# A two-layer mLSTM and latent-attention trunk: gate columns beside v, the rotary key's two parts in one weight tile, the mLSTM chunk's fp32 products by fours

## The chip, the cores and the metric

The kernel runs on one core of one Trainium2 chip. The metric is the device time of one execution in microseconds (us). Times of several executions are given as their median with the lowest and the highest.

## The reference, cut to what matters

The input is one sequence of S = 1024 tokens with D = 1024 features, all in fp32. Layer A is an mLSTM mixer (8 heads, query and key width 64, value width 128, chunks of 128 tokens) with a squared-ReLU MLP behind it. From its output comes a shared key and value: a latent of 256 features and a rotary key of 64. Layer B is latent attention over that, and an MLP again. Norms and a modulation by a conditioning vector stand around every part. The change touches two places of it, the mLSTM mixer:

```python
def mlstm_mixer(h, w_in, gate_b, head_g, w_out):
    proj = h @ w_in    # q 512, k 512, v 1024, i gate 8, f gate 8, o gate 1024 columns
    q, k, v, ig, fg, og = jnp.split(proj, splits, axis=-1)
    i_pre, f_pre = (ig + gate_b[0]), (fg + gate_b[1])
    hh = mlstm_chunkwise(q, k, v, i_pre, f_pre)
    ...
def step(carry, xs):         # one chunk of 128 tokens, per head
    ...
    s = jnp.einsum('bhtd,bhsd->bhts', qb, kb) * w_intra
    num = (w_inter[..., None] * jnp.einsum('bhtd,bhde->bhte', qb, C)   # from the state
           + jnp.einsum('bhts,bhse->bhte', s, vb))                     # within the chunk
    den = w_inter * jnp.einsum('bhtd,bhd->bht', qb, n) + jnp.sum(s, axis=-1)
    h = num / jnp.maximum(jnp.abs(den), jnp.exp(-m_t))[..., None]
```

and the rotary key of the shared latent:

```python
    kv = modulate(rmsnorm(x, g_in), shift, scale) @ w_a
    c_kv, k_rope = jnp.split(kv, [B_KV_LORA], axis=-1)    # 256 and 64 columns
    k_rope = apply_rope(k_rope, cos, sin)                 # x1 cos - x2 sin, x2 cos + x1 sin
```

## The kernel before

**Tiles and precision.** The tokens are worked in two halves of 512 (`hfs[0]`, `hfs[1]`), features on the partitions for the most part. Large products are made exact to about fp32 by splitting each operand into a rounded part `hi` and a rest `lo` and adding three products, lo by hi, hi by lo and hi by hi (`mm3`, L233 to L236). Weights are loaded by `wload`: SyncE's queue fetches 512 KB into one of four `raw` buffers (L214), ScalarE (ACT) rounds them into `wh` (L192), and VectorE (DVE) forms the rest `wl` (L193); eight `ws` buffers hold the two.

**Memory.** PSUM is shared by three pools: `ps` and `pc` with two banks each, and `pm` with two pairs of banks. In SBUF the temporaries are `tmc` (six of 512 columns), `tmp` (three) and `tma` (one), and the larger tiles `k4` (24) and `hd` (8).

**Order.** A scheduler places the instructions on in-order engine queues from the order in which they are traced. That order is woven by hand from generators: `weave` and `weave_n` run so many steps of one beside each step of another, `with_bg` runs steps of a background beside a stage, and `in_turn` alternates two streams. The background (`bgs`) computes the modulation vectors: `ada_chunk` loads 512 KB at a time into `raw` (L356) and multiplies and adds on DVE into the one `tma` tile (L361, L363). `prompt` and `tc.high_priority` move an operation ahead in the schedule, and `tc.issue_after` holds one back.

**The mLSTM's first half** (L1730 to L1742). `qk_pairs` (L572) makes q and k in four blocks of 256 features, the last of them at its end (L600 to L610), from eight weight blocks. `gates_in` (L612) then loads the 16 gate columns, spreads hi and lo over one weight tile of 128 columns (rows 0, 32 for hi and 64, 96 for lo of the result) and makes 16 products of 512 columns (L628, L629) into a `ps` bank. `gates0` (L681) adds hi and lo rows on DVE and runs a chain of some 30 short operations of DVE and ACT on eight rows: log-sigmoid, cumulative sums, running maximum, weights. `v_in` (L643) makes v with tokens on the partitions: four blocks of 256 columns, for each the two weight loads and four token tiles of 24 products of 256 columns. Beside it runs `intra0` (L743), which makes each head pair's decay weights (L754 and L757 on PE, L761 on ACT), the 64-row products of key and query (L769), their product with the weights (L774) and the scaling of q (L777 on PE, L778 on DVE).

**The chunks.** `chunks0` (L796) takes four chunks for each half. Two heads are the two row groups of 64 of one product. For each of two `pm` pairs (q), and each of its two head pairs (i), it traces two products with the state `Cst` (64 rows of contraction each, L813), then two products within the chunk (128 rows, L818), and so on alternately. The first chunk of all has no state. Behind these come the transposes of the keys (L826), the norm on ACT and DVE (L837 to L850, which frees the `pm` pair), the state's update (L861, 64 columns of output side by side) and the transposes of the result (L876). In the first half they alternate with the output gate's projection `og0` and steps of `norm0`, the second half's first norm; in the second half with `wout` of the first. `rms_x1` (L516) sums squares for that norm on ACT; the squares themselves are thrown away, into a `pc` bank.

**The second half of the mLSTM** (L1745 to L1752) runs `gates_in` with no background, then q and k in eight blocks of 128 (`qk_in`) and v, with `intra0` woven in at 0.8 steps of it to each step, and the background at 1.7.

**The rotary key.** `latent_weights` (L1133) folds gains into the latent's weights in advance, in the background, splits them, and stores hi and lo in DRAM (`lw[b, i]`); block 2 is the rotary key's 64 columns, twice side by side. `latent` (L1162) loads the blocks (`load`), makes each by `proj` (24 products of 512 columns), multiplies with the tokens' norm (`scaled`, L1212) and adds a bias (`based`, L1216). `rope` (L1113) splits block 2, multiplies by the cosines, turns the halves by two products with a permutation (L1123, L1124), multiplies by the sines and adds. The same `rope` serves the queries.

Of the kernel before, what the change touches and what calls it, by code (L numbers as in the profile page):

```python
# [9 lines left out]
F32 = mybir.dt.float32  # L10
F32R = mybir.dt.float32r
# [6 lines left out]
P = 128  # L18
# [64 lines left out]
def kernel(  # L83
# [66 lines left out]
    def pc():  # L150
        return pp.tile([P, 512], F32, tag="pc", bufs=2, name=f"pc_{next(uid)}")
# [420 lines left out]
    def qk_pairs(hf, w0, ahead):  # L572


        h = hf.h
        hf.q = [k4v(), k4v()]
        hf.k = [k4v(), k4v()]
        m0, m1 = pm(), pm()
        acc = [(m0[:, 0], m0[:, 1]), (m1[:, 0], m1[:, 1]), (ps(), ps())]

        def half(b, kh, w):
            for r in range(2):
                for k in range(4):
# [16 lines left out]
        acc.append((ps(), ps()))  # L600
        w = [w_qk(3, 0), w_qk(3, 1)]
        for r in range(2):
            for kk in range(KD):
                wk, k = w[kk // 4], kk % 4
                mm3(
                    acc[3][r], wk[0][:, k, ts(r, P)], wk[1][:, k, ts(r, P)], h.hi[kk], h.lo[kk],
                    kk == 0, kk == KD - 1,
                )
            qk_evac(hf, 6 + r, acc[3][r])
            yield  # L610

    def gates_in(hf):  # L612
        h = hf.h
        wg = raw(F32R).rearrange("p (a b) -> p a b", b=P)
        nc.gpsimd.memset(wg.bitcast(F32), 0.0)
        rg = tmp()
        rgv = rg[:, :128].rearrange("p (k n) -> p k n", n=16)
        nc.sync.dma_start(rgv, wcols(w_in, 2048, 16))
        for g in range(2):
            s = ts(g, 8)  # L620
            nc.scalar.copy(wg[:, :, 32 * g : 32 * g + 8], rgv[:, :, s])
            nc.vector.tensor_sub(
                wg[:, :, 64 + 32 * g : 72 + 32 * g], rgv[:, :, s],
                wg[:, :, 32 * g : 32 * g + 8].bitcast(F32),
            )
        gp = ps()
        for k in range(KD):
            nc.tensor.matmul(gp, wg[:, k], h.lo[k], start=k == 0, stop=False)  # L628
            nc.tensor.matmul(gp, wg[:, k], h.hi[k], start=False, stop=k == KD - 1)  # L629
        hf.gp = gp  # L630
        yield from gates0(hf)
        yield
# [9 lines left out]

    def v_in(hf):  # L643
        h = hf.h
        hf.v = []
        for t in range(4):
            v = k4().rearrange("p (h e) -> p h e", e=VE)
            nc.gpsimd.memset(v[:, :, 128:VE], 1.0)
            hf.v.append(v)
# [31 lines left out]
    def gates0(hf):  # L681
# [1 line left out]
        gp, half = hf.gp, hf.i  # L683
        r8 = lambda: tmc()[0:8]
        t1, t2, t3 = r8(), r8(), r8()
        nc.vector.tensor_copy(t1, gp[64:72])
# [109 lines left out]
    def chunks0(hf):  # L796
# [4 lines left out]
        for j in range(4):  # L801
            g = hf.i * 4 + j
            cs = ts(j, P)
            v = hf.v[j]
            nvs = []
            for q in range(2):
                num = pm()
                nv = num[:, :, 0 : 2 * VE].rearrange("p b (i e) -> p b i e", e=VE)
                for i in range(2):
                    p_ = 2 * q + i  # L810

                    for r in range(2 if g > 0 else 0):
                        nc.tensor.matmul(  # L813
                            nv[:, r, i], hf.q[p_ // 2][ts(r, 64), p_ % 2, cs],
                            Cst[ts(r, 64), p_], start=True, stop=False,
                        )
                    for r in range(2):
                        nc.tensor.matmul(  # L818
                            nv[:, r, i], hf.PT[p_][:, r, cs], v[:, 2 * p_ + r],
                            start=g == 0, stop=True,  # L820
                        )
                nvs.append(nv)
            if g < 7:
                pt = pc()
                for p_ in range(4):
# [280 lines left out]

    perm = selW[:, 0]

    def rope_perm():
        for q in range(4):  # L1110
            nc.vector.tensor_copy(perm[:, ts(q, 32)], ident[:, ts(q ^ 1, 32)])

    def rope(pt, hf, b=None):  # L1113

        hi, lo, t1 = tmc(F32R), tmc(F32R), tmc()
        split_mod(hi, lo, pt, b)
        if b is None:
            nc.vector.tensor_mul(t1, pt, hf.cs[:, 0])
        else:
            nc.vector.scalar_tensor_tensor(t1, pt, b, hf.cs[:, 0], ALU.add, ALU.mult)  # L1120
        yield
        p2 = pc()
        nc.tensor.matmul(p2, perm, lo, start=True, stop=False)  # L1123
        nc.tensor.matmul(p2, perm, hi, start=False, stop=True)  # L1124
        t2 = tmc()
        nc.vector.tensor_mul(t2, p2, hf.cs[:, 1])
        nc.vector.tensor_add(t1, t1, t2)
        return t1

# [3 lines left out]
    def latent_weights():  # L1133
# [4 lines left out]
        for b, vs in enumerate(views):  # L1138
# [19 lines left out]
            nc.vector.reduce_sum(lbias[:, b : b + 1], pt[:, :P], axis=AX.X)  # L1158

    kkd = scratch([2, P, H], "kkd")  # L1160

    def latent(hf, behind):  # L1162
# [5 lines left out]
        def load(b):  # L1168
            with tc.high_priority(PRIO):
                w = []  # L1170
                for i in range(2):
                    t = raw(F32R)
# [11 lines left out]
        def proj(b):  # L1184
            if b < 4:
                load(b + 2)
            w, pt = ready.pop(0), pc() if b == 2 else ps()
            for k in range(KD):
                mm3(pt, w[0][:, k], w[1][:, k], h.hi[k], h.lo[k], k == 0, k == KD - 1)
            return pt  # L1190

        lb = lambda b: lbias[:, b : b + 1]
# [777 lines left out]
```

## Time and profile before

| | |
|---|---|
| timed runs | 2396.66 us, median of 3 (2395.84 to 2397.26) |
| profiled execution | 2392.8 us |
| its span | 2391.0 us |
| mean granted clock of TensorE | 0.999 |
| instructions in the span | 30521 |
| HBM traffic | 313.24 MB read, 59.24 MB written |
| DMA | mean 157 GB/s |

The profile shows one execution. PE stands for TensorE's matmuls, PEld for its weight loads, DVE for VectorE, ACT for ScalarE, POOL for GpSimd, SP for SyncE and SPq for its queue of DMA issues. A row of a timeline reads: start, duration, engine, line of the kernel, operation, output and inputs by tile names, the product's rows and columns of TensorE, output or operand size, type, and how many instructions run together in that row; the brackets at its end say how long the engine had been idle and on what it waited. Records of PE overlap, since matmuls are pipelined. A granted clock of 1.00 is full speed. Busy shares are means over stages with different limits.

### The profile page before, as it was taken

The numbers are of one execution on the slowest core, as the hardware profiler recorded it, in microseconds if no ns is written. First come the engines' busy times: TensorE is split into PE (matmuls) and PEld (weight loads), VectorE is DVE, ScalarE is ACT, GpSimd is POOL, SyncE is SP. The second block draws the span as 40 slices with busy tenths as digits, with TensorE's granted clock in tenths as the row PEclk, the third lists the DMA queues.
The fourth block names the chain that finished last, engine by engine and source line by source line (L and its number), as shares of the span: only waits on it lengthen the run. The fifth ranks groups of instructions, "written<-read, shape, count | busy, mean of one in ns | idle before, by whom it ended". The sixth has DMA issues, their size and how long they took to land.

```text
span 2391.0 us, 30521 instructions
## 1 busy us (share of the span) xinstructions
PE 2365.1 (99%) x11621; PEld 1945.3 (81%) x11621; DVE 1549.9 (65%) x2431; ACT 1055.2 (44%) x1712; POOL 18.2 (1%) x91
## 2 busy tenths in 40 slices
PE   8999999999999999999999999999999999999998
PEld 5888888888888887888888878888888888888886
DVE  6667866868656677877764867766666395353345
ACT  4355334655333454444444554444444353444333
POOL 1000000000000000000000000000000000000000
PEclk9999999999999999999999999999999999999999
DMA  8442654545555745545543444774434354354431
GB/s 311 150 142 81 195 175 142 158 133 159 185 167 158 238 141 178 164 156 185 169 138 113 155 163 153 259 242 135 137 98 154 103 166 134 102 183 141 145 98 62
DMA packets 377106, 374.48 MB, mean 157 GB/s; under 512 B 24355, under 2 KB 282464, under 8 KB 376960
## 3 DMA queue, kind: packets, MB, share of 16 engines
q1 hardware_dynamic: 376672, 372.44, 49.0%
q8 instruction: 91, 1.49, 0.3%
q14 instruction: 55, 0.45, 0.1%
q0 software_dynamic: 288, 0.10, 0.0%
HBM read 313.24 MB, written 59.24 MB: 156 GB/s over the span
## 4 chain that ended last, share of the span: by engine, by line
PE 92%; DVE 3%; DMA 3%; ACT 1%; issue 1%; SPq 0%; DVEq 0%; ACTq 0%
PE ps L234 17%; PE ps L236 16%; PE ps L235 16%; PE pm L234 10%; PE pm L235 10%; PE pm L236 10%; PE pc L1448 1%; PE pc L234 1%; PE pc L235 1%; PE pc L236 1%; PE pm L1334 1%; PE pm L818 1%; DMA raw<-in_mlp_w_dram 1%; DMA raw<-in_a_w_in_dram 1%; PE pm L1328 1%
## 5 line engine op out<-in xcount | busy, mean ns | idle before, releaser
L193 DVE TENSOR_TENSOR wl<-raw,wh 128x1024 fp32r<-128x1024 f32 (+2 forms) x366 | 438.7, 1202 | 437.4 <-ACT wh L192 428.5
L192 ACT CAST wh<-raw 128x1024 fp32r<-128x1024 f32 (+2 forms) x366 | 376.3, 1032 | 708.8 <-PE ps L234 385.0
L234 PE MATMUL ps<-k,wl 128*128 128x512 f32 x1496 | 598.3, 400 | 0.9 <-DVE wl L193 0.8
L236 PE MATMUL ps<-k,wh 128*128 128x512 f32 x1496 | 588.8, 394 | 0.0
L235 PE MATMUL ps<-k,wh 128*128 128x512 f32 x1496 | 587.1, 392 | 0.0
L236 PEld LDWEIGHTS ps<-k,wh 128*128 128x128 f32 x1496 | 280.9, 188 | 66.5 <-issue 0.2
L234 PEld LDWEIGHTS ps<-k,wl 128*128 128x128 f32 x1496 | 281.0, 188 | 65.9 <-issue 2.7
L235 PEld LDWEIGHTS ps<-k,wh 128*128 128x128 f32 x1496 | 281.4, 188 | 62.2 <-issue 1.4
L201 DVE TENSOR_TENSOR k<-k,pm 128x512 f32<-128x512 f32 (+1 forms) x254 | 211.1, 859 | 107.5 <-PE pm L236 107.0
L234 PE MATMUL pm<-hd,wl 128*128 128x512 f32 x512 | 201.5, 394 | 0.4 <-ACT hd L473 0.4
L235 PE MATMUL pm<-hd,wh 128*128 128x512 f32 x512 | 199.6, 390 | 0.2 <-DVE hd L474 0.2
L236 PE MATMUL pm<-hd,wh 128*128 128x512 f32 x512 | 199.7, 390 | 0.0
L234 PE MATMUL pm<-wh,hd 128*128 128x512 f32 x488 | 193.1, 396 | 2.0 <-ACT raw L1340 1.6
L235 PE MATMUL pm<-wl,hd 128*128 128x512 f32 x488 | 191.4, 392 | 0.0
L236 PE MATMUL pm<-wh,hd 128*128 128x512 f32 x488 | 190.4, 390 | 0.0
L363 DVE SCALAR_TENSOR_TENSOR tma<-raw,cond,tma 128x512 f32<-128x512 f32 x168 | 125.6, 748 | 20.1 <-DMA raw<-in_kv_ada_w_dram 13.5
L474 DVE TENSOR_TENSOR hd<-tmp,hd 128x512 fp32r<-128x512 f32 x128 | 88.3, 690 | 57.0 <-ACT hd L473 56.7
L1340 ACT ACTIVATE raw<-pm,sm 128x128 f32<-128x128 f32 (+3 forms) x64 | 47.5, 742 | 151.3 <-DVE sm L1339 129.2
L235 PEld LDWEIGHTS pm<-hd,wh 128*128 128x128 f32 x512 | 96.2, 188 | 21.2 <-DVE hd L474 0.5
L234 PEld LDWEIGHTS pm<-hd,wl 128*128 128x128 f32 x512 | 96.1, 188 | 21.3 <-ACT hd L473 0.8
L236 PEld LDWEIGHTS pm<-hd,wh 128*128 128x128 f32 x512 | 96.1, 188 | 20.8
L960 ACT ACTIVATE tmp<-ps 128x512 f32<-128x512 f32 x128 | 75.8, 592 | 83.5 <-PE ps L236 83.4
(348 smaller groups left out, 3489.4 us busy)
## 6 DMA issues: line engine op xcount, KB each, us to landing
raw<-in_mlp_w_dram SPq DMA_DIRECT2D x256, 512.0 KB, 4.1
raw<-in_ada_w_dram SPq DMA_DIRECT2D x80, 512.0 KB, 4.4
raw<-in_a_w_in_dram SPq DMA_DIRECT2D x48, 512.0 KB, 4.0
xs<-k SPq DMA_DIRECT2D x40, 256.0 KB, 4.6
raw<-in_kv_ada_w_dram SPq DMA_DIRECT2D x16, 512.0 KB, 3.8
raw<-in_a_w_out_dram SPq DMA_DIRECT2D x16, 512.0 KB, 4.2
kd<-k SPq DMA_DIRECT2D x32, 256.0 KB, 3.8
vd<-k SPq DMA_DIRECT2D x32, 256.0 KB, 4.5
```

Source lines behind the costliest of these rows:

```text
L192: nc.scalar.copy(hi[:, :n], r[:, :n])
L193: i = nc.vector.tensor_sub(lo[:, :n], r[:, :n], hi[:, :n].bitcast(F32))
L201: return f(*a, **k)
L234: nc.tensor.matmul(o, ll, rh, start=start, stop=False)
L235: nc.tensor.matmul(o, lh, rl, start=False, stop=False)
L236: pe_last[0] = nc.tensor.matmul(o, lh, rh, start=False, stop=stop)
L363: nc.vector.scalar_tensor_tensor(acc, r[:, kk], cond[:, k : k + 1], acc, ALU.mult, ALU.add)
L474: nc.vector.tensor_sub(lo, u, hi.bitcast(F32))
L818: nc.tensor.matmul(nv[:, r, i], hf.PT[p_][:, r, cs], v[:, 2 * p_ + r], start=g == 0, stop=True,)
L960: nc.scalar.activation(s, pt, AF.Relu)
L1328: nc.tensor.matmul(o[:, :w], ql, kh, start=True, stop=False)
L1340: nc.scalar.activation(pr[:, :n], f, AF.Exp, bias=m, scale=SCALE, accum_out=l)
```

## The change

It has three parts, and four edits that go with them.

Gates beside v: `gates_in` now makes v's last 256 columns and the 16 gate columns together, in products of 272 columns with tokens on the partitions (three weight loads, of three, three and two blocks of 128 rows). ACT copies v's part and the gate's part out; four fp32 transposes of 64 columns, into rows 0 to 63 of a `pc` bank, bring the gates back to one row for each head. `gates0` then opens with three DVE operations where it had five. `v_in` keeps three blocks. The last block of q and k becomes `qk_last`, behind `gates_in`, with the background beside it.

Rotary key: hi stands in columns 0 to 63 of the one weight tile, lo in 64 to 127, so that 16 products make block 2. The sum of the two parts and the turn are made by four products with two matrices, `both` and `both_perm`, in `rope_key`. Blocks 0 and 1 of the latent are first copied out of PSUM by ACT.

Chunks: both `pm` pairs are taken at the start of a chunk; four products with the state come together, then four within the chunk, twice over. The sums are the same.

Further: the squares of `rms_x1` go to a `tmc` tile, and the weaving rates go from 1.5 to 2.5 in the first half and from 1.7 and 0.8 to 1.5 and 0.95 in the second.

```diff
@@ rms_x1
-                junk = pc()
+                junk = tmc()
@@ qk_pairs: its last block leaves, as
+    def qk_last(hf):
+        h, acc = hf.h, (ps(), ps())
         w = [w_qk(3, 0), w_qk(3, 1)]
...
@@ gates_in
-        wg = raw(F32R).rearrange("p (a b) -> p a b", b=P)
...
-        for k in range(KD):
-            nc.tensor.matmul(gp, wg[:, k], h.lo[k], start=k == 0, stop=False)
-            nc.tensor.matmul(gp, wg[:, k], h.hi[k], start=False, stop=k == KD - 1)
+        n = 272
+        ws_ = [
+            wload([(0, 0, wcols(w_in, 1792, n, k0, nk))], n) for k0, nk in ((0, 3), (3, 3), (6, 2))
+        ]
+        g = tmc()[:, :256].rearrange("p (t a b) -> p t a b", a=2, b=32)
+        nc.gpsimd.memset(g[:, :, :, 8:32], 0.0)
+        for t in range(4):
+            pt = ps()[:, :n]
+            for k in range(KD):
+                w = ws_[k // 3]
+                mm3(
+                    pt, h.hi[k][:, ts(t, P)], h.lo[k][:, ts(t, P)],
+                    w[0][:, k % 3], w[1][:, k % 3], k == 0, k == KD - 1,
+                )
+            evac(hf.v[t][:, 6:8, 0:128], pt[:, 0:256].rearrange("p (a b) -> p a b", b=P))
+            evac(g[:, t, :, 0:8], pt[:, 256:272].rearrange("p (a b) -> p a b", b=8))
+            yield
+        gp = pc()
+        for t in range(4):
+            nc.tensor.transpose(
+                gp[0:64, ts(t, P)], g[:, t].rearrange("p a b -> p (a b)"), ident
+            )
         hf.gp = gp
         yield from gates0(hf)
@@ v_in
-        for j in range(4):
+        for j in range(3):
@@ gates0
-        nc.vector.tensor_copy(t1, gp[64:72])
-        nc.vector.scalar_tensor_tensor(t1, gp[0:8], col(GB, 1)[0:8], t1, ALU.add, ALU.add)
-        nc.vector.tensor_copy(t2, gp[96:104])
+        nc.vector.tensor_scalar(t1, gp[0:8], col(GB, 1)[0:8], None, ALU.add)
         nc.vector.tensor_copy(t3, gp[32:40])
-        nc.vector.scalar_tensor_tensor(t2, t3, col(GB + 1, 1)[0:8], t2, ALU.add, ALU.add)
+        nc.vector.tensor_scalar(t2, t3, col(GB + 1, 1)[0:8], None, ALU.add)
@@ chunks0
-            nvs = []
-            for q in range(2):
-                num = pm()
...
+            nvs = [
+                pm()[:, :, 0 : 2 * VE].rearrange("p b (i e) -> p b i e", e=VE) for q in range(2)
+            ]
+            for i in range(2):
+                for q in range(2 if g > 0 else 0):
                     for r in range(2):
                         nc.tensor.matmul(
+                            nvs[q][:, r, i], hf.q[q][ts(r, 64), i, cs],
+                            Cst[ts(r, 64), 2 * q + i], start=True, stop=False,
+                        )
+                for q in range(2):
+                    for r in range(2):
+                        p_ = 2 * q + i
+                        nc.tensor.matmul(
+                            nvs[q][:, r, i], hf.PT[p_][:, r, cs], v[:, 2 * p_ + r],
                             start=g == 0, stop=True,
                         )
@@ rope_perm, rope_key
+            nc.vector.tensor_add(both[:, s], ident[:, s], ident[:, ts(q ^ 2, 32)])
+            nc.vector.tensor_add(both_perm[:, s], ident[:, ts(q ^ 1, 32)], ident[:, ts(q ^ 3, 32)])
...
+    def rope_key(u, hf, b):
+        hi, lo, t1, t2 = tmc(F32R), tmc(F32R), tmc(), tmc()
+        split_mod(hi, lo, u, b)
+        yield
+        for t, w, i in ((t1, both, 0), (t2, both_perm, 1)):
+            p = pc()
+            nc.tensor.matmul(p, w, lo, start=True, stop=False)
+            nc.tensor.matmul(p, w, hi, start=False, stop=True)
+            nc.vector.tensor_mul(t, p, hf.cs[:, i])
         nc.vector.tensor_add(t1, t1, t2)
         return t1
@@ latent_weights
-                nc.sync.dma_start(lw[b, i], t.bitcast(F32))
+                if b == 2:
+                    f = lambda t: t.rearrange("p (a b) -> p a b", b=P)[:, :, ts(i, 64)]
+                    nc.sync.dma_start(f(lw[b, 0]), f(t).bitcast(F32))
+                else:
+                    nc.sync.dma_start(lw[b, i], t.bitcast(F32))
...
@@ latent: load, proj, scaled
+                if b == 2:
+                    nc.tensor.matmul(pt, w[0][:, k], h.lo[k], start=k == 0, stop=False)
+                    nc.tensor.matmul(pt, w[0][:, k], h.hi[k], start=False, stop=k == KD - 1)
+                else:
+                    mm3(pt, w[0][:, k], w[1][:, k], h.hi[k], h.lo[k], k == 0, k == KD - 1)
...
+            if m < 2:
+                evac(o, pt)
+                pt = o
...
-        rp = rope(scaled(tmc(), 2), hf, lb(2))
+        rp = rope_key(scaled(tmc(), 2), hf, lb(2))
@@ the main sequence
     drain(with_bg(gates_in(hfs[0]), bgs, 1))
+    drain(with_bg(qk_last(hfs[0]), bgs, 1))
     x1 = load_x1()
-    drain(weave(with_bg(v_in(hfs[0]), bgs, 1), intra0(hfs[0]), 1.5))
+    drain(weave(with_bg(v_in(hfs[0]), bgs, 1), intra0(hfs[0]), 2.5))
...
-    drain(weave_n(with_bg(main, bgs, 1.7), intra0(hfs[1]), 0.8))
+    drain(weave_n(with_bg(main, bgs, 1.5), intra0(hfs[1]), 0.95))
```

More of the change, by code (lines that the diff above doesn't have):

```diff
@@ L605, in qk_pairs @@
                 mm3(
-                    acc[3][r], wk[0][:, k, ts(r, P)], wk[1][:, k, ts(r, P)], h.hi[kk], h.lo[kk],
+                    acc[r], wk[0][:, k, ts(r, P)], wk[1][:, k, ts(r, P)], h.hi[kk], h.lo[kk],
                     kk == 0, kk == KD - 1,
                 )
-            qk_evac(hf, 6 + r, acc[3][r])
+            qk_evac(hf, 6 + r, acc[r])
             yield
@@ L613, in gates_in @@
         h = hf.h
-        wg = raw(F32R).rearrange("p (a b) -> p a b", b=P)
[L615 to L624, printed above, removed]
-            )
-        gp = ps()
-        for k in range(KD):
-            nc.tensor.matmul(gp, wg[:, k], h.lo[k], start=k == 0, stop=False)
-            nc.tensor.matmul(gp, wg[:, k], h.hi[k], start=False, stop=k == KD - 1)
+        hf.v = []
+        for t in range(4):
+            v = k4().rearrange("p (h e) -> p h e", e=VE)
+            nc.gpsimd.memset(v[:, :, 128:VE], 1.0)
+            hf.v.append(v)
+        n = 272
[16 more added lines that the diff above has]
+        gp = pc()
+        for t in range(4):
+            nc.tensor.transpose(
+                gp[0:64, ts(t, P)], g[:, t].rearrange("p a b -> p (a b)"), ident
+            )
         hf.gp = gp
@@ L644, in v_in @@
         h = hf.h
[L645 to L649, printed above, removed]
-        for j in range(4):
+        for j in range(3):
             w0 = wload([(0, 0, wcols(w_in, 1024 + j * 256, 256, 0, 4))], 256)
@@ L804, in chunks0 @@
             v = hf.v[j]
-            nvs = []
-            for q in range(2):
-                num = pm()
[L808 to L816, printed above, removed]
+            nvs = [
[3 more added lines that the diff above has]
+                for q in range(2 if g > 0 else 0):
                     for r in range(2):
                         nc.tensor.matmul(
-                            nv[:, r, i], hf.PT[p_][:, r, cs], v[:, 2 * p_ + r],
+                            nvs[q][:, r, i], hf.q[q][ts(r, 64), i, cs],
[6 more added lines that the diff above has]
+                            nvs[q][:, r, i], hf.PT[p_][:, r, cs], v[:, 2 * p_ + r],
                             start=g == 0, stop=True,
                         )
-                nvs.append(nv)
             if g < 7:
@@ L1107, with rope @@
     perm = selW[:, 0]
+    both, both_perm = selW[:, 1], selW[:, 2]
     def rope_perm():
         for q in range(4):
-            nc.vector.tensor_copy(perm[:, ts(q, 32)], ident[:, ts(q ^ 1, 32)])
-    def rope(pt, hf, b=None):
-        hi, lo, t1 = tmc(F32R), tmc(F32R), tmc()
[L1116 to L1120, printed above, removed]
+            s = ts(q, 32)
+            nc.vector.tensor_copy(perm[:, s], ident[:, ts(q ^ 1, 32)])
+            nc.vector.tensor_add(both[:, s], ident[:, s], ident[:, ts(q ^ 2, 32)])
+            nc.vector.tensor_add(both_perm[:, s], ident[:, ts(q ^ 1, 32)], ident[:, ts(q ^ 3, 32)])
+    def rope(pt, hf):
+        hi, lo, t1 = tmc(F32R), tmc(F32R), tmc()
+        split_mod(hi, lo, pt, None)
+        nc.vector.tensor_mul(t1, pt, hf.cs[:, 0])
         yield
@@ L1126, in rope @@
         nc.vector.tensor_mul(t2, p2, hf.cs[:, 1])
+        nc.vector.tensor_add(t1, t1, t2)
+        return t1
+    def rope_key(u, hf, b):
[7 more added lines that the diff above has]
+            nc.vector.tensor_mul(t, p, hf.cs[:, i])
         nc.vector.tensor_add(t1, t1, t2)
@@ L1157, in latent_weights @@
             nc.tensor.transpose(pt[:, :P], acc, ident)
-            nc.vector.reduce_sum(lbias[:, b : b + 1], pt[:, :P], axis=AX.X)
+            n = 64 if b == 2 else P
+            nc.vector.reduce_sum(lbias[:n, b : b + 1], pt[:n, :P], axis=AX.X)
+            if n < P:
+                nc.vector.memset(lbias[n:P, b : b + 1], 0.0)
     kkd = scratch([2, P, H], "kkd")
@@ L1170, in load @@
                 w = []
-                for i in range(2):
-                    t = raw(F32R)
+                for i in range(1 if b == 2 else 2):
+                    t = raw(F32R) if i else None
                     if i == 0:
```

2 lines of the change are left out of this document (removed).

## The prediction, made before the changed kernel ran

> **What bounds the kernel now.** I read the page first: its first line, the row of engines, and the chain of work that ended last.
>
> ```profile
> span 2391.0 us, 30521 instructions
> ...
> PE 2365.1 (99%) x11621; PEld 1945.3 (81%) x11621; DVE 1549.9 (65%) x2431; ACT 1055.2 (44%) x1712; POOL 18.2 (1%) x91
> ...
> PE 92%; DVE 3%; DMA 3%; ACT 1%; issue 1%; SPq 0%; DVEq 0%; ACTq 0%
> ```
>
> PE is busy for 99% of the span and is 92% of the last chain, so a product taken off PE shortens the span unless PE then waits. The profiled execution took 2392.8 us around this span of 2391.0 us, the median of the timed runs is 2396.66 us: the sum is made on the first and carried to the second, 3.9 us higher. Next, the waits of PE over the whole span, longest first:
>
> ```profile
> PE pc L530 <- DMA k<-in_x_dram: 3.8, 4, 1.4
> ...
> PE ps L234 <- DVE wl L193: 0.8, 1, 0.8
> PE pc L754 <- ACT tmc L761: 0.5, 1, 0.5
> ```
>
> Behind the start, nothing holds PE for even 1.7 us in total under one name. Then the stages that the change touches, window by window (columns: length, then busy time of PE, PEld, DVE, ACT and POOL, granted clock, DMA share, GB/s):
>
> ```profile
> 83.00:110.00 27.00, 27.00 (x229) 25.69 (x228) 20.07 (x42) 6.84 (x17) 0.00 (x0) 1.00 0.10 32
> 110.00:125.00 15.00, 14.46 (x113) 12.19 (x112) 12.90 (x21) 8.82 (x22) 0.00 (x0) 1.00 0.73 227
> 125.00:145.00 20.00, 19.55 (x161) 18.91 (x160) 12.78 (x27) 11.63 (x33) 0.00 (x0) 1.00 0.73 199
> 250.00:270.00 20.00, 19.25 (x123) 14.78 (x123) 14.22 (x26) 8.43 (x21) 0.00 (x0) 1.00 0.72 215
> ```
>
> PE idles 0.54 + 0.45 + 0.75 = 1.7 us here. The first row is the odd one: DMA at a tenth while DVE is at three quarters. This is the one place where a wait is near, and I come back to it.
>
> **A product costs its start-to-start distance**, not its duration, since records overlap. The timeline of PE gives the distances (columns: start, duration, then line and tiles):
>
> ```profile
> 61.63 0.40 PE L234 MATMUL ps<-k,wl 128*128 128x512 f32 x1
> ...
> 78.79 0.39 PE L628 MATMUL ps<-k,raw 128*128 128x512 f32 x1
> 79.02 0.40 PE L629 MATMUL ps<-k,raw 128*128 128x512 f32 x1
> ...
> 82.60 0.93 PE L769 MATMUL pm<-k,k 64*128 64x128 f32 x10
> ...
> 87.82 0.28 PE L234 MATMUL ps<-wh,k 128*128 128x256 f32 x1
> 87.94 0.28 PE L235 MATMUL ps<-wl,k 128*128 128x256 f32 x1
> 88.05 0.28 PE L236 MATMUL ps<-wh,k 128*128 128x256 f32 x1
> ```
>
> 512 columns take 0.23 us and 256 take 0.118 us: 0.44 ns a column. All 16 gate products of a half take 82.60 - 78.79 = 3.81 us.
>
> **Gates beside v.** Both halves lose the 16 products, 2 x 3.81 = 7.6 us. In exchange the 96 products of v's last block in each half go from 256 to 272 columns: 16 x 0.44 = 7 ns each, 192 x 0.007 = 1.3 us; bounds: nothing, and a full 512 columns (rival B). Eight fp32 transposes of 64 gate columns are new. Their nearest rows are the transposes of 128 columns and the one product that also has 64 output rows:
>
> ```profile
> 345.34 1.04 PE L876 MATMUL pc<-ident,tmc 128*128 128x128 f32 x8
> 346.31 0.49 PE L813 MATMUL pm<-Cst,k 64*128 64x130 f32 x4
> ...
> 374.08 0.39 PE L236 MATMUL ps<-k,wh 128*128 128x512 f32 x1
> 374.40 1.11 PE L861 MATMUL pc<-k,tmc 128*64 128x130 f32 x16
> 375.44 0.50 PE L234 MATMUL ps<-k,wl 128*128 128x512 f32 x1
> ```
>
> L876: 0.97 us for eight, 0.11 each with the change of tile mode after them. L861 is entered 0.32 us after a 512-column product instead of 0.23, and eight of its two-record products take 1.04 us, of which about 0.2 is no product time: a run of such work costs some 0.3 us beside the work. In the built order of the changed kernel the eight transposes stand in four runs (three and one in each half): 8 x 0.11 + 4 x 0.3 = 2.1 us, bounds 0.9 (no cost of runs) and 4.7 (rival D). Gates together: -7.6 + 1.3 + 2.1 = **-4.2 us**.
>
> At this place the Trainium skill speaks against the change: TensorEngine Tiling (Array Packing), section Restrictions and Gotchas, says that column tiling excludes the transpose mode for fp32 on TRN2, and TensorE: Matmul & The Clock Gate, section Terms, calls that mode four times faster for fp32. An estimate from those pages: 0.44 us a transpose, 2.6 us more for eight. No run here shows a transpose into 64 rows; by the rule the sum would be 2.6 us smaller.
>
> **Rotary key in one tile.** In both halves 24 products of 512 columns become 16, and the two turning products become four: 6 fewer, 12 in all. The distance there is that of every 512-column product:
>
> ```profile
> 911.80 0.40 PE L1123 MATMUL pc<-tmc,selW 128*128 128x512 f32 x1
> 912.04 0.40 PE L1124 MATMUL pc<-tmc,selW 128*128 128x512 f32 x1
> 912.28 0.39 PE L235 MATMUL ps<-k,lw 128*128 128x512 f32 x1
> ```
>
> 12 x 0.23 = **-2.8 us**. The other edits there (one weight load of 512 KB less each time, two copies by ACT, a few small DVE operations in the setup) lie beside PE at 99%; ACT at 44% hides them. If that cover failed, the two copies would cost 0.6 us each per half.
>
> **Products by fours.** Nothing is removed; the state's products of two heads (64 rows each, side by side) and the full products within the chunk now come four at a time over both PSUM pairs. One chunk of the second half now, and the nearest rows of longer runs:
>
> ```profile
> 346.31 0.49 PE L813 MATMUL pm<-Cst,k 64*128 64x130 f32 x4
> 346.73 0.71 PE L818 MATMUL pm<-k,hd 128*128 128x130 f32 x4
> 347.38 0.49 PE L813 MATMUL pm<-Cst,k 64*128 64x130 f32 x4
> ...
> 350.49 0.60 PE L826 MATMUL pc<-ident,k 128*128 128x128 f32 x4
> ...
> 112.00 0.71 PE L769 MATMUL pm<-k,k 64*128 64x128 f32 x8
> 112.65 0.39 PE L754 MATMUL pc<-identb,maskA 128*128 128x512 bf16 x1
> ...
> 144.23 1.06 PE L818 MATMUL pm<-k,hd 128*128 128x130 f32 x8
> 145.12 0.60 PE L826 MATMUL pc<-ident,k 128*128 128x128 f32 x4
> ```
>
> A run of two state products (four records) takes 0.42 us, while a run of four such half-height products (eight records, L769) takes 0.65: joining two saves 0.84 - 0.65 = 0.19 us. Two within-chunk products take 0.65 us between two runs of the state; four take 0.89 with no change of tile mode before them, and about 0.2 more with both changes: 1.30 - 1.09 = 0.21 us. So each joint saves 0.40 us. Ideally there are 7 chunks x 2 joints; in the built order the runs of state products fall from 31 to 18, for norm0's transposes stand between some of them: 13 x 0.40 = 5.2, and I take **-5.0 us**, bounds 0 (accumulating over four banks doesn't run on) and -5.6 (14 joints). The first chunk has no state and stays.
>
> The new wait: the first product into the second PSUM pair comes two runs earlier. Behind it on PE stands all of the chunk. The pair is free when DVE has scaled the chunk before:
>
> ```profile
> 360.76 0.69 DVE L850 TENSOR_TENSOR tmc<-pm,sm 128x512 f32<-128x512 f32 x1
> ...
> 364.18 0.49 PE L813 MATMUL pm<-Cst,k 64*128 64x130 f32 x4
> ```
>
> It is free at 361.45, and the chunk starts at 364.18: 2.7 us of cover, so nothing; without the cover, some 1 us a chunk.
>
> **What moves.** The gates' chain on DVE now starts behind four tiles of v, with qk's last block beside it; intra0 is woven with fewer v steps, and its short products (L769) stand in three more runs: 3 x 0.2 = +0.6 us. What may come late is v's weights. SyncE issues in order. Its longest wait (total, times, longest), and then the timeline, for the third block of v:
>
> ```profile
> SPq L214 <- DVE tma L363: 31.5, 5, 26.2
> ```
>
> ```profile
> 82.71 0.68 DVE L686 COPY tmc<-ps 8x512 f32<-8x512 f32 x1 [1.88 <-PE ps L629]
> ...
> 109.43 2.71 SPq L214 DMA_DIRECT2D raw<-in_a_w_in_dram  x2
> ...
> 117.37 1.22 DVE L193 TENSOR_TENSOR wl<-raw,wh 128x1024 fp32r<-128x1024 f32 x1
> ```
>
> The load sat 26.2 us behind a DVE operation of the background's (L363), which DVE did after the gates' chain: that is the idle DMA of the window from 83 to 110. In the changed order the load so held is that of v's second block. Its chain starts near 79 instead of 82.7 (qk's block begins at 61.6; four tiles of 24 x 0.125, three transposes, 0.8 us of L769 and four of qk's steps), has two of five opening copies less (-2.1 us) and one weight split more (+1.1); the background's operation behind it ends near 97, the loads land 4 us later, and with 1.05 us of ACT and 1.2 us of DVE each the second half is whole near 106. PE wants it at 105: 26 us of products behind the chain's start (8 us of qk, 11.3 of v, 5 of intra0, 1.5 of the next block's first half). A wait of 1 to 2 us, where 1.0 us of idling stood in the two windows from 110 to 145: I take **+1.0 us**, bounds -1.7 (all idling goes) and +8 (rival A).
>
> **Sum.** -4.2 - 2.8 - 5.0 + 0.6 + 1.0 = -10.4 us: 2392.8 to 2382.4 for a profiled execution, 2396.66 to **2386.3 us** for the median.
>
> **Rivals.**
> A, late weights. The hold on SyncE stays as long as now, counted from the chain's start: 26.7 us to the first load, so 105.5, whole near 113 instead of 105: 8 us of waiting in place of 1. That gives -3.4 us, 2393.3 us. For it: DVE at three quarters in that window; against: the chain has fewer operations, and the second half has no background in its gates.
> B, slower. A product of 272 columns takes as long as one of 512: 192 x (0.230 - 0.125) = +20.2 us, so +9.8, 2406.5 us. It turns the sign once 272 columns take over 0.125 + 10.4 / 192 = 0.179 us. Against it: 256 and 512 columns lie on one line through the origin but for 6 ns.
> C, the fours bring nothing: -5.4 us, 2391.3 us. For it: the accumulation over four banks has no row here; against: L769 changes PSUM regions too and gains.
> D, transposes into 64 rows without the fast mode, as a mechanism of this kernel: each streams its 128 columns four times, 4 x 0.11 us: -7.8 us, 2388.9 us. The two pages above are its rule.
>
> **How the numbers follow.** Forecast 0.70, A 0.10, B 0.04, C 0.06, D 0.10. The range takes all but B and the late ends of A: the low end has the transposes at 0.9, all 14 joints and no idling (-4.2 - 1.2 - 2.8 - 5.6 + 0.6 - 1.7 = -14.9), 2381.7; the high end is rival A's 2393.3. 0.2% is 4.8 us, about what a measurement can tell. Faster by more: the forecast, D, most of C, little of A: 0.84. Within: the rest of C and nearly all of A: 0.11. Slower: B and something unforeseen: 0.05.
>
> **What would show it.** In the profile after: no L628 rows of 512 columns in the gates; 272-column products 0.125 us apart; the four runs of 64-row transposes at 0.3 to 0.8 us; clean chunks of the second half from 4.18 us (346.31 to the start of L826 at 350.49) to about 3.4; 16 products for the key. Wrong would be a window between 95 and 125 with PE under its length by more than 3 us, or products of 272 columns over 0.14 us apart.

## The result, and the profile after

The changed kernel takes 2385.86 us (median of 6 runs, 2384.99 to 2388.66) where the kernel before takes 2396.96 us (6 runs, 2395.84 to 2399.38): a ratio of 0.9958, with a 95% interval of 0.9947 to 0.9969, or 11.1 us less. The forecast was 2386.3, 10.4 less.

The first lines of the page after:

```profile
span 2386.9 us, 30478 instructions
...
PE 2356.2 (99%) x11585; PEld 1939.7 (81%) x11585; DVE 1542.5 (65%) x2430; ACT 1057.0 (44%) x1726; POOL 17.0 (1%) x91
...
PE 85%; DMA 6%; DVE 5%; ACT 2%; issue 2%; SPq 0%; DVEq 0%; ACTq 0%
```

PE still bounds the kernel and makes 36 products fewer: 32 in the gates and 12 in the key are gone, and 8 transposes have come. The two profiled spans differ by only 4.1 us, 2391.0 to 2386.9, though the medians differ by 11.1. The waits of PE in the changed kernel's profiled execution (total, times, longest) show a part of it:

```profile
PE pm L1370 <- DMA k<-td: 2.4, 1, 2.4
PE pc L343 <- DVE tma L363: 1.6, 2, 1.0
...
PE ps L234 <- ACT k L676: 0.8, 1, 0.8
PE pc L785 <- ACT tmc L769: 0.7, 1, 0.7
```

The first two stand outside of the stages that the change touches; the run e4_again below shows what they are. First those stages, in the same windows as before:

```profile
83.00:110.00 27.00, 27.00 (x179) 23.25 (x178) 22.29 (x42) 7.70 (x14) 0.00 (x0) 1.00 0.53 176
110.00:125.00 15.00, 15.00 (x121) 12.96 (x121) 10.47 (x19) 7.39 (x22) 0.00 (x0) 1.00 0.49 147
125.00:145.00 20.00, 18.50 (x150) 17.31 (x149) 15.82 (x38) 14.02 (x40) 0.00 (x0) 1.00 0.74 206
...
250.00:270.00 20.00, 20.00 (x104) 15.13 (x103) 11.75 (x27) 5.80 (x14) 0.00 (x0) 1.00 0.09 27
```

DMA is at 0.53 in the first window, where it was at 0.10. PE idles 1.5 us in these windows, all of it between 125 and 145, where it idled 1.7 before, spread over three. The gates of the first half, on the timeline of PE:

```profile
81.81 0.29 PE L234 MATMUL ps<-wh,k 128*128 128x272 f32 x1
81.93 0.29 PE L235 MATMUL ps<-wl,k 128*128 128x272 f32 x1
82.06 0.29 PE L236 MATMUL ps<-wh,k 128*128 128x272 f32 x1
82.18 0.49 PE L642 MATMUL pc<-ident,tmc 128*64 128x128 f32 x3
82.43 0.48 PE L234 MATMUL ps<-k,wl 128*128 128x512 f32 x1
82.74 0.40 PE L235 MATMUL ps<-k,wh 128*128 128x512 f32 x1
...
86.35 0.27 PE L642 MATMUL pc<-ident,tmc 128*64 128x128 f32 x1
86.38 0.47 PE L235 MATMUL ps<-k,wh 128*128 128x512 f32 x1
86.69 0.39 PE L236 MATMUL ps<-k,wh 128*128 128x512 f32 x1
```

Products of 272 columns stand 0.12 to 0.13 us apart. Three transposes into 64 rows take 0.25 us, 0.08 each, and the product behind a run of them is followed after 0.31 us where 0.23 is usual. Next a chunk of the second half, and the second and the last of the 16 key products:

```profile
340.56 0.72 PE L820 MATMUL pm<-Cst,k 64*128 64x130 f32 x8
341.20 1.16 PE L827 MATMUL pm<-k,hd 128*128 128x130 f32 x8
342.29 0.72 PE L820 MATMUL pm<-Cst,k 64*128 64x130 f32 x8
342.94 1.16 PE L827 MATMUL pm<-k,hd 128*128 128x130 f32 x8
343.94 0.60 PE L834 MATMUL pc<-ident,k 128*128 128x128 f32 x4
...
893.99 0.39 PE L1223 MATMUL pc<-k,lw 128*128 128x512 f32 x1
...
897.24 0.39 PE L1223 MATMUL pc<-k,lw 128*128 128x512 f32 x1
```

The chunk's products take 343.94 - 340.56 = 3.38 us, where they took 4.18. Each row stands for eight records, four products.

### The profile page after: what moved, and what is told of

Read it like the earlier page. It is cut to its first block, busy times and chain, and to the rows that moved or that the text cites. A ratio compares the mean times of both kernels' runs of the same rounds, so it can differ in the third digit from the quotient of the medians.

```text
span 2386.9 us, 30478 instructions
## 1 busy us (share of the span) xinstructions
PE 2356.2 (99%) x11585; PEld 1939.7 (81%) x11585; DVE 1542.5 (65%) x2430; ACT 1057.0 (44%) x1726; POOL 17.0 (1%) x91
## 4 chain that ended last, share of the span: by engine, by line
PE 85%; DMA 6%; DVE 5%; ACT 2%; issue 2%; SPq 0%; DVEq 0%; ACTq 0%
PE ps L234 16%; PE ps L235 15%; PE ps L236 15%; PE pm L234 9%; PE pm L235 9%; PE pm L236 9%; DMA raw<-in_mlp_w_dram 4%; DVE wl L193 1%; PE pc L1488 1%; ACT wh L192 1%; DVE tma L363 1%; PE pm L1374 1%; PE pc L234 1%; PE pc L235 1%; PE pc L236 1%
## 5 line engine op out<-in xcount | busy, mean ns | idle before, releaser
L193 DVE TENSOR_TENSOR wl<-raw,wh 128x1024 fp32r<-128x1024 f32 (+3 forms) x368 | 439.2, 1197 | 446.5 <-ACT wh L192 444.0
L192 ACT CAST wh<-raw 128x1024 fp32r<-128x1024 f32 (+3 forms) x368 | 376.8, 1028 | 731.6 <-PE ps L234 374.2
L234 PE MATMUL ps<-k,wl 128*128 128x512 f32 x1496 | 597.8, 400 | 1.0 <-DVE wl L193 0.9
L234 PEld LDWEIGHTS ps<-k,wl 128*128 128x128 f32 x1496 | 281.0, 188 | 65.9 <-issue 2.7
L234 PE MATMUL pm<-hd,wl 128*128 128x512 f32 x512 | 201.5, 394 | 0.4 <-ACT hd L473 0.4
L234 PE MATMUL pm<-wh,hd 128*128 128x512 f32 x488 | 192.5, 394 | 1.7 <-ACT raw L1380 1.3
L363 DVE SCALAR_TENSOR_TENSOR tma<-raw,cond,tma 128x512 f32<-128x512 f32 x168 | 125.5, 747 | 25.5 <-DMA raw<-in_kv_ada_w_dram 13.3
L234 PEld LDWEIGHTS pm<-hd,wl 128*128 128x128 f32 x512 | 96.1, 188 | 21.9 <-ACT hd L473 0.8
L234 PEld LDWEIGHTS pm<-wh,hd 128*128 128x128 f32 x488 | 91.6, 188 | 23.0 <-ACT raw L1380 3.8
```

Of the source, the lines that this page charges most:

```text
L192: nc.scalar.copy(hi[:, :n], r[:, :n])
L193: i = nc.vector.tensor_sub(lo[:, :n], r[:, :n], hi[:, :n].bitcast(F32))
L234: nc.tensor.matmul(o, ll, rh, start=start, stop=False)
L363: nc.vector.scalar_tensor_tensor(acc, r[:, kk], cond[:, k : k + 1], acc, ALU.mult, ALU.add)
```

## The experiments

Each kernel was timed beside the kernel before. A difference in us is worked out from the ratio: its distance from 1 times 2395.3, the median of the kernel before in these runs.

**The three parts alone.** On the kernel before, e1_gates has the hunks of `gates_in`, `qk_last`, `v_in`, `gates0`, `rms_x1` and the three rates; e2_key those of `rope_key`, `latent_weights` and `latent`; e3_fours that of `chunks0`, as in the diff above.

> Only the gates' part on the kernel before: gate columns beside v, the last block of q and k behind them, the squares of the second half's norm in SBUF, the three weaving rates; key and chunks as before. By the prediction's terms: -7.6 for the 16 products of each half, +1.3 for 272 columns, +2.1 for the transposes, +0.6 for intra0 in more runs, +1.0 of waits: -2.6 us, ratio 0.9989. If late weights (rival A) were the true price: +4 us. If 272 columns were billed as 512 (rival B): +17 us. If the transposes into 64 rows were four times slower (rival D): 0 us. In the profile: 272-column products 0.125 us apart by the forecast, over 0.18 by B; a run of the new transposes 0.3 to 0.4 us for three by the forecast, 1.3 us by D.

Measured: 2389.01 us, ratio 0.9973 (0.9963 to 0.9984), -6.5 us with an interval of -8.9 to -3.8. All four prices fall, the forecast's -2.6 too: the part gives more than that, by 1 us at least. It has the rates and the squares in it.

> Only the rotary key's part on the kernel before: 12 products of 512 columns fewer in all. By the prediction 12 x 0.23 = -2.8 us, ratio 0.9988. Rival: PE finds a wait where the products were (the copies by ACT, the bias and split of the key, or loads that do not come earlier than now), and the time stays: 0 us. In the profile, the first tells itself by PE idling no more between the latent's first product and the queries' than before, the rival by a named wait of 1 us or more there in each half.

Measured: 2391.92 us, ratio 0.9989 (0.9980 to 0.9998), -2.6 us against the -2.8 expected. The rival shows in part: between 393 and 970 us PE now has one wait, `PE ps L234 <- DVE wl L193` of 0.4 us, where it had none.

> Only the chunks' part on the kernel before: products by fours over both PSUM pairs. The built order has 18 runs of state products where 31 were: by the prediction 13 x 0.40 = -5.2 us, ratio 0.9978, and a clean chunk of the second half at 3.4 us where it was 4.18. By rival C (the accumulation over four banks brings nothing) 0 us and a chunk at about 4.2. If the earlier need of the second pair costs a wait, PE idles ahead of the state products for up to 1 us a chunk: +2 us in place of -5.

Measured: 2390.32 us, ratio 0.9980 (0.9971 to 0.9989), -4.8 us against -5.2. Rival C falls, and no wait on the second PSUM pair shows.

The parts sum to -13.9 us, the whole is -11.1, or -11.5 in the next run. Of this gap, 1.6 us are counted twice: gates and key alone each have 29 runs of state products where the kernel before has 31, but all three together have the 18 of the fours alone (2 x 2 x 0.40). The rest is no more than the intervals leave open. The traces say where the gap lies: from the last product within a chunk of the first half to the last one of the second, the kernel before takes 182.5 us, gates, key and fours alone 4.6, 1.7 and 3.8 less, which makes 10.0, and the changed kernel (e4_again) only 7.2 less.

**The changed kernel once more.**

> The changed kernel unaltered, once more, since its first profiled execution was 2388.66 us beside a median of 2385.86, and that of the kernel before 2392.8 beside 2396.96: the profiled pair differ by 4.1 us, the medians by 11.1. If these 7 us are a matter of single executions (a lower granted clock in the first 60 us, a load or two landing later), this profiled execution comes at 2385 to 2387, the median again at 2386, and PE's wait of 2.4 us for the transposed keys' load of the first attention block is gone or smaller. If they belong to the change, the wait for that load stands again near 2.4 us, with the slow products behind it.

Measured: 2383.59 us, ratio 0.9952 (0.9939 to 0.9964); its profiled execution took 2383.59 too. The wait for the same load:

```profile
PE pm L1370 <- DMA k<-td: 0.5, 1, 0.5
```

So the 7 us are of single executions, as the first theory had it. They stand in four places. PE's waits for L363, 1.6 us in the changed kernel's first profile, are gone in e4_again. In that first profile the load stood open for 2.4 us, and in the runs shown here for 0.4 to 2.4, with no regard to the change: 2.2 in e1_gates, 0.4 in the kernel before. Behind the wait of 2.4 us the products are slow, which costs another 1.5 us; the changed kernel's PE in its first profile:

```profile
1577.16 0.39 PE L1369 MATMUL pm<-k,k 128*128 128x512 f32 x1
1579.91 0.50 PE L1370 MATMUL pm<-hd,k 128*128 128x512 f32 x1 [2.36 <-DMA k<-td]
...
1582.64 0.63 PE L1369 MATMUL pm<-k,k 128*128 128x512 f32 x1
1583.06 0.63 PE L1370 MATMUL pm<-hd,k 128*128 128x512 f32 x1
1583.49 0.58 PE L1371 MATMUL pm<-hd,k 128*128 128x512 f32 x1
1583.90 0.39 PE L1374 MATMUL pm<-k,k 128*128 128x512 f32 x1
```

And the start, which the change doesn't touch before 60 us; first the kernel before, then the changed one in its first profile (the column before the last two is the granted clock), with the product that stands at 61.63 in the kernel before:

```profile
25.00:30.00 5.00, 4.29 (x11) 2.04 (x11) 4.87 (x8) 3.57 (x5) 0.00 (x0) 0.66 1.05 388
...
41.00:45.00 4.00, 4.00 (x19) 3.27 (x18) 3.87 (x6) 2.58 (x4) 0.00 (x0) 1.00 1.05 344
```

```profile
25.00:30.00 5.00, 4.39 (x9) 2.13 (x11) 4.87 (x9) 3.57 (x5) 0.00 (x0) 0.50 1.05 387
...
41.00:45.00 4.00, 4.00 (x12) 3.13 (x12) 3.74 (x7) 2.57 (x5) 0.00 (x0) 0.57 1.06 345
```

```profile
63.77 0.40 PE L234 MATMUL ps<-k,wl 128*128 128x512 f32 x1
```

By this product of the opening stage the changed kernel stands 2.1 us later. From it to PE's last product, the first profile of the changed kernel takes 6.5 us less than the kernel before, and e4_again 11.7 less, close to the difference of the medians. The profiled execution of the kernel before was a lucky one: its mean clock was 0.999, and of 24 executions of that kernel beside e1 to e4 only two had that, 21 had 0.997 or less. The medians are the result, and not the pair of profiles.

**Products by eights.**

```diff
@@ chunks0
             for i in range(2):
                 for q in range(2 if g > 0 else 0):
...
-                            Cst[ts(r, 64), 2 * q + i], start=True, stop=False,
+                            Cst[ts(r, 64), 2 * q + i], start=i == 0, stop=False,
+            for i in range(2):
                 for q in range(2):
...
-                            start=g == 0, stop=True,
+                            start=g == 0 and i == 0, stop=i == 1,
```

> The changed kernel, with the chunk's products by eights: all eight products with the state (only the first into each bank starts it), then all eight within the chunk. The built order has 10 runs of state products where the changed kernel has 18. If a joint saves 0.40 us, as the prediction has it, 8 x 0.40 = -3.2 us against the changed kernel, about -14.5 against the kernel before, ratio 0.9939, and a clean chunk of the second half some 0.4 us shorter than with fours. If the gain came from spreading over both PSUM pairs and not from fewer changes, nothing more: ratio 0.9954, and the same chunk.

Measured: 2380.69 us, ratio 0.9940 (0.9926 to 0.9954), -14.4 us: 2.9 less than e4_again, 3.2 expected. The chunk of the second half in e5_eights:

```profile
336.50 1.16 PE L819 MATMUL pm<-Cst,k 64*128 64x130 f32 x16
337.60 2.06 PE L827 MATMUL pm<-k,hd 128*128 128x130 f32 x16
339.49 0.60 PE L834 MATMUL pc<-ident,k 128*128 128x128 f32 x4
```

These are 2.99 us, 0.39 less than by fours, for one change from 64-row to 128-row products and back. Dose and effect agree: 4.18, 3.38 and 2.99 us with four, two and one runs of state products, over two PSUM pairs in the last two. What pays is the run, and not the number of banks.

**The rates alone, and the rate of the first half.** On the kernel before:

```diff
-                junk = pc()
+                junk = tmc()
@@ the main sequence
-    drain(weave(with_bg(v_in(hfs[0]), bgs, 1), intra0(hfs[0]), 1.5))
+    drain(weave(with_bg(v_in(hfs[0]), bgs, 1), intra0(hfs[0]), 2.5))
...
-    drain(weave_n(with_bg(main, bgs, 1.7), intra0(hfs[1]), 0.8))
+    drain(weave_n(with_bg(main, bgs, 1.5), intra0(hfs[1]), 0.95))
```

> On the kernel before, only the three weaving rates and the squares of the second half's norm in SBUF. The gates' part alone gave 6.3 us where the terms of the prediction sum to 2.6. If the surplus comes from the rates and the squares, this gives -3 to -4 us, ratio 0.9985. If it comes from the gates' own products and transposes being cheaper than they were priced, this gives 0 to -1 us. The built order has 30 runs of state products where 31 were, and 13 of the short products of key and query where 15 were: by 0.40 and 0.2 us -0.8 us, ratio 0.9997.

Measured: 2402.62 us, ratio 1.0029 (1.0018 to 1.0041), 7 us **slower**. Both expectations miss. The hold on SyncE, then rows of DVE, of PE, and the window, each of e6_rates; between DVE and PE the row of the kernel before for the same operation (L363):

```profile
SPq L214 <- DVE tma L363: 39.7, 5, 33.4
```

```profile
112.19 0.69 DVE L774 TENSOR_TENSOR hd<-pm,tmc 128x512 f32<-128x512 f32 x1 [2.81 <-ACT tmc L761]
113.85 0.69 DVE L774 TENSOR_TENSOR hd<-pm,tmc 128x512 f32<-128x512 f32 x1 [0.97 <-ACT tmc L761]
...
117.19 2.32 DVE L363 SCALAR_TENSOR_TENSOR tma<-raw,cond,tma 128x512 f32<-128x512 f32 x3
```

```profile
108.65 0.75 DVE L363 SCALAR_TENSOR_TENSOR tma<-raw,cond,tma 128x512 f32<-128x512 f32 x1
```

```profile
118.60 0.50 PE L777 MATMUL pc<-RM,selW 128*128 128x512 f32 x1 [0.74 <-ACT tmc L761]
119.63 0.38 PE L754 MATMUL pc<-identb,maskA 128*128 128x512 bf16 x1 [0.53 <-ACT tmc L761]
...
122.73 0.80 PE L234 MATMUL ps<-wh,k 128*128 128x256 f32 x2 [1.11 <-DVE tma L363]
```

```profile
110.00:125.00 15.00, 12.03 (x81) 8.99 (x79) 11.18 (x20) 7.82 (x26) 0.00 (x0) 0.87 0.32 90
```

This is rival A of the prediction, in another kernel. Two more of intra0's products on DVE (L774) now stand ahead of the background's L363, and DVE, in order, idles for the exponentials of ACT (2.81 and 0.97 us) before it comes to it: at 117.19, where the kernel before began it at 108.65. The load of v's weights stands behind that for 33.4 us where it was 26.2, PE has only intra0's products left, waits on them in turn, and idles 3.0 us in 15 with a clock of 0.87. Rival A was priced at 8 us of waiting. Here it is about half of the 7: from the opening's product above to the last product within a chunk of the first half, e6_rates takes 3.7 us more than the kernel before. Another 1.0 us is in the second half, whose own rates e6_rates has too, and 2.6 us between there and the latent, of which 1.8 are one wait for L363 as in the changed kernel's first profile. No run has the second half's rates alone. In the changed kernel the longest hold of a load of v's weights behind L363 is shorter; its SyncE row, and the start of the gates' chain on DVE:

```profile
SPq L214 <- DVE tma L363: 21.9, 6, 13.0
```

```profile
86.66 0.74 DVE L696 TENSOR_SCALAR tmc<-pc,cols 8x512 f32<-8x512 f32 x1 [2.84 <-PE pc L642]
```

So the part called gates takes away half of that hold, though its chain starts later than before (86.66 against 82.71). That it therefore bears a rate that the kernel before does not is likely, and not shown by itself. What the rate costs it:

```diff
-    drain(weave(with_bg(v_in(hfs[0]), bgs, 1), intra0(hfs[0]), 2.5))
+    drain(weave(with_bg(v_in(hfs[0]), bgs, 1), intra0(hfs[0]), 1.5))
```

> The changed kernel with the first half's weaving rate back at 1.5. The built order has 16 runs of state products, 18 within the chunk and 18 of key and query, where the changed kernel has 18, 17 and 19: by the prices of the prediction -0.5 to -1 us against the changed kernel, ratio to the kernel before about 0.995. If the rate of 2.5 is what keeps v's weights or the decay weights in time, PE idles by 1 to 3 us more between 95 and 145 us, ratio 0.9965.

> The gates' part on the kernel before as in the first run, but with the first half's weaving rate left at 1.5. The new rates alone cost 7.2 us on the kernel before, where a load of v's weights stood 33.4 us behind DVE's background operation, and the gates' part with them gave 6.3. If the gates' part itself shortens that hold and the rate of 2.5 takes some of it back (2.7 us between the changed kernel and its rate of 1.5), this gives -9 us, ratio 0.9962, with the two waits of PE near 133 and 139 us gone. If the rate matters only where the chunks go by fours, it gives -6.3 us as before, ratio 0.9973.

e7_rate_1_5, on the changed kernel: 2380.86 us, ratio 0.9939 (0.9926 to 0.9952), 2.7 us less than e4_again (1.9 less than e8_rows128 below, the same order of products) and more than the 0.5 to 1 expected. e9_gates_1_5, the gates' part alone: 2387.98 us, ratio 0.9970 (0.9959 to 0.9982), -7.2 us where e1_gates has -6.5; between the two expectations, and their intervals overlap. In both, the waits `PE ps L234 <- ACT k L676` and `PE pc L785 <- ACT tmc L769` (0.8 and 0.7 us) are gone and one, `PE pc L869 <- ACT tmp L498`, of 0.5 us has come, so 1.0 us less of idling is shown. The whole gain of e7 is in the first half: from the opening's product to the last one within a chunk it takes 136.5 us, where three profiles of the changed order of products (e8_rows128 among them) take 138.3 to 139.0. Two runs of state products less (16 for 18) would be 0.8 us by the price of a joint; the rest is not settled.

**Transposes into 128 rows.** In the changed kernel:

```diff
-        g = tmc()[:, :256].rearrange("p (t a b) -> p t a b", a=2, b=32)
+        g = tmc().rearrange("p (t a b) -> p t a b", a=2, b=64)
...
-                gp[0:64, ts(t, P)], g[:, t].rearrange("p a b -> p (a b)"), ident
+                gp[:, ts(t, P)], g[:, t].rearrange("p a b -> p (a b)"), ident
...
```

> The changed kernel with the gate tile padded to 128 columns, so that its eight transposes fill 128 rows in place of 64; the order of the products is the same. If transposes into 64 rows fall out of a fast mode (rival D, and the rule of the Trainium skill beside it), three of them in a run take some 1 us less here than in the changed kernel, 2.6 us in all. If both run alike, the run of three takes the same to 0.1 us, and the times are the same to within 1 us.

Measured: 2382.75 us, ratio 0.9948 (0.9934 to 0.9962), e4_again within 1 us. The same place in e8_rows128:

```profile
82.12 0.49 PE L642 MATMUL pc<-ident,tmc 128*128 128x128 f32 x3
82.37 0.48 PE L234 MATMUL ps<-k,wl 128*128 128x512 f32 x1
```

0.25 us for three, as into 64 rows. Rival D falls, and with it what the prediction took from the Trainium skill, TensorEngine Tiling (Array Packing), section Restrictions and Gotchas: the exclusion named there costs these transposes nothing.

**Both gains together.** The changed kernel by eights with the rate at 1.5, and at 1.0:

> The changed kernel with products by eights and the first half's rate at 1.5, each of which gave some 3 us alone. The built order has 11 runs of state products, 12 within the chunk. If the two add up, 2396 - 14.6 - 2.9 = about 2378 us, ratio 0.9927. If both act on one wait of the first half (the two that stood near 133 and 139 us), no more than one of them: 0.994.

> As the run before, with the rate at 1.0, so that fewer steps of the decay weights stand beside v and more behind it. If the waits of the first half all come from DVE's and ACT's work for the decay weights being put ahead of v's weights, this is no slower than at 1.5. If the decay weights then come late behind v, PE waits on ACT's exponentials (tmc) by 1 to 4 us, ratio 0.9935 to 0.9945.

e10_best: 2380.64 us, ratio 0.9936 (0.9924 to 0.9949). They do not add: in its trace one wait, `PE ps L234 <- ACT k L676` of 1.1 us, stands in the first half again, where e7_rate_1_5 has none. e11_best_1_0: 2382.44 us, ratio 0.9944 (0.9930 to 0.9957), at the slow end of its second expectation. The three best (e5, e7, e10) can't be told apart; each beats the changed kernel by about 3 us.

## Why the prediction came out right, step by step

- **The bound** holds: PE stays at 99%, and what left PE left the time.
- **Key**, -2.8: -2.6 measured, in part by luck. Two runs of state products fewer (31 to 29) are in it, 0.8 us by the price of a joint. In the first latent, from block 0's first product to the first with the attention mask, e2_key is 0.8 us shorter (87.17 against 87.97) where six products are 1.4: a wait of 0.4 us was costed at nothing.
- **Fours**, -5.0: -4.8 measured; the chunk was to take "about 3.4" and takes 3.38. The price of a joint, 0.40 us, was worked out from runs of other lines, and the eights confirm it at 0.39.
- **Gates**, -4.2, with +0.6 and +1.0 beside it -2.6: **-6.5** measured. This is the part that was mis-sized. (1) "a run of such work costs some 0.3 us beside the work": a run of these transposes costs the 0.08 us that the next product is longer. That makes two runs a half 0.25 + 0.03 + 2 x 0.08 = 0.44 us, 0.9 in all against the 2.1 taken, just the lower bound. The 0.3 had been read from L861, whose two-record products are another kind of work. (2) The wait: +1.0 was taken, and PE idles 1.5 us where it idled 1.7, so -0.2. (3) 0.8 us came from state products that happen to be joined in the new order (31 to 29 runs), which no step had. Together -1.2 - 1.2 - 0.8 = -3.2 of the 3.9 between forecast and measurement. (4) Another 1.2 us, which more than closes the rest, stands where nothing was changed: from the last product with the attention mask to PE's last one, the same 2460 products without a wait take 554.2 us in the kernel before, e2_key, e3_fours and e6_rates, and 553.0 in every kernel with the gates' part. Why they stand closer is not known.
- **v's weights.** The place was right, the picture of it was not. The chain was to start near 79 and starts at 86.66: the fourth transpose (at 86.35) stands behind 13 products of qk's last block and a run of L777, which the working left out. The chain's opening got 1.8 us shorter (from 3.7 to 1.9) where 2.1 was taken. Both the demand and the supply moved with it, and no wait for weights came.
- **The rates** were not priced at all, but for intra0's +0.6 us (in the trace its short products take 12.7 us in 19 runs where they took 11.8 in 15, so +0.9). Together with the squares they cost 7 us on the kernel before, 3.7 of it in the first half; the first half's rate alone costs some 2 to 3 us on the changed one.
- **Sum.** The terms missed 3.9 us in the gates, and 2.4 to 2.8 us of the parts' gains are not in the whole, 1.6 of them by overlap. 10.4 against 11.1 is thus closer than its steps were.
- **The time that was carried** from a profiled execution to the median (3.9 us) was sound as a difference; some 2 us of it are the start above, whose low clock is the usual one by the 24 executions.
- **Rivals.** B falls by the rows of 272 columns, C by e3_fours and e5_eights, D by e8_rows128. A did not come, but it exists: the kernel before pays some 4 us for it in e6_rates.

## What to carry to other kernels

Short products of different tile shapes are priced by the run: count the runs in the built order before and after, price a joint from the nearest rows, and go on joining while accumulation allows it. A rate of weaving is an edit like any other; ask which DMA stands on its queue behind an operation that the rate delays. Where effects are of 0.1 to 0.5%, time parts alone, and compare one profile with another only from a common product on.

## What the runs showed of the hardware

A wait of PE can cost more than its length. Behind 2.36 us of idling the products of the changed kernel stood 0.43 us apart instead of 0.23 from 1580.5 to 1583.9, and behind 2.21 us in e1_gates in the same way; behind 1.30 us in e3_fours they ran at full rate at once, and so they did behind 1.83 us in e6_rates (at 711.83). The slow stretch costs 1.5 us: from L1370 at 1579.91 to L1374 at 1583.90 are 3.99 us, and 2.46 for the same products in e3_fours. The granted clock of the changed kernel there:

```profile
1580.00:1585.00 5.00, 5.00 (x21) 4.26 (x22) 0.98 (x2) 0.89 (x2) 0.00 (x0) 0.66 1.03 417
```

Several short waits do it too. In e6_rates PE idled four times for 0.53 to 1.11 us between 117.9 and 122.7, and then made 256-column products 0.21 us apart instead of 0.12:

```profile
118.00:122.00 4.00, 1.90 (x5) 0.75 (x5) 3.96 (x8) 1.95 (x8) 0.00 (x0) 0.89 0.63 158
122.00:127.80 5.80, 5.07 (x22) 4.97 (x23) 5.20 (x9) 5.80 (x18) 0.00 (x0) 0.50 0.77 246
```

The slow stretch of 3.4 us behind a single wait is the length that the Trainium skill gives for the activity window, in TensorE: Matmul & The Clock Gate, part 1 (What's actually happening). The same page of the Trainium skill, under HAM oscillation, asks for no idle gaps over about 3.4 us; in these runs a single gap of 2.2 us was enough and one of 1.8 was not.
